# The opening of TensorE in a hybrid mLSTM / attention layer: pinned order, unread products, and the value product between the modulation visits

## The chip, the core and the metric

The kernel runs on one core of a Trainium2 chip. The metric is the device time of one execution in microseconds (us). Of the core's engines, TensorE (PE in the rows; PEld are its weight loads) multiplies, VectorE (DVE), ScalarE (ACT) and GpSimd (POOL) work element by element, and SyncE (SP) issues most of the DMAs. Each engine takes its instructions in the order in which they stand in its queue.

## The reference, cut to what matters

One layer for 512 latent and 128 context tokens, together 640 columns of 1024 features. Only its opening is touched:

```python
mod = (jax.nn.silu(cond) @ w_ada + b_ada)[..., None, :]
sh1, sc1, g1, sh2, sc2, g2 = jnp.split(mod, 6, axis=-1)
h = _rmsnorm(x, norm1_g) * (1 + sc1) + sh1
mq, mk, mv, mo, gates, q_lat, kv_lat, k_rope = _split_cols(h @ w_in, IN_SIZES)
...
```

Behind it come the mLSTM heads, latent attention, the output product and the MLP.

## The kernel before, in words

All matrices are float32. Large products are made of three: a matrix is split into a rounded high part and the low rest, and high x high, low x high and high x low are summed (`mm3`). The splits of weights are `split` (L109 on ScalarE makes the high part `wh`, L110 on VectorE or GpSimd the low part `wl`). Features lie in eight blocks of 128 (k = 0 to 7), tokens in five tiles of 128.

The opening runs so. SyncE fetches x in four pieces, then the first 2048 columns of `w_ada` in eight blocks (`ad`, 1 MB each) with the first weights `st` of the value product between them. ScalarE squares x (L448), VectorE adds the squares in pairs (L449), and TensorE takes their means over features in four groups of five products (`n_pc`, L452; each float32 product of the program shows as two in the trace). GpSimd takes the power -1/2 (`rs`, L361), and TensorE spreads the result over partitions (`n_pb`, L437).

The modulation of the first normalisation comes in four visits, g = 0 to 3. A visit is 16 narrow products (`ada`, L389, "the strips"), a copy of their result by ScalarE (`m`, L394), two products that add the strips up ("the sums", L397), and on VectorE `modT` (L400) and the gain `acol` (L475, L476). Visit g serves blocks k = 2g and 2g+1: VectorE makes `h` (L480), ScalarE its high part `hh` (L481), VectorE its low part `hl` (L482).

Then `group_n` gives the value product `mv`: for each k and each of five tiles the three products L486, L487, L488, 120 in all; after it the product `kv`, 120 again. The program lists the visits first and `mv` after them, and a scheduler, which works with times of its own, sets the order on each engine: what is ready first by its times goes first. Staging tiles `st` come from two buffers, the parts `wh` and `wl` from three each, so the first `kv` weights (`st` of `w_kv`) are fetched into the buffer that the third `mv` pair of blocks leaves once its low part is made.

Of the kernel before, what the change touches and what calls it, by code (L numbers as in the profile page):

```python
# [1 line left out]

# [1 line left out]

# [15 lines left out]
P = 128  # L20
D = 1024
KT = D // P
# [4 lines left out]
NT = T // P  # L27
# [17 lines left out]
ORDER = ("M1", "M6", "M7", "M5", "M2", "M4", "M3")  # L45
ORDER0 = ("M1", "M5", "M2", "M6", "M7", "M4", "M3")
PRE = 4
AHEAD = 2
LAST = 1
OUT_ORDER = (0, 4, 1, 5, 2, 6, 3, 7)  # L50
# [4 lines left out]
def hybrid_layer(ctx: ExitStack, tc: tile.TileContext, d, o):  # L55
    nc = tc.nc
    V, S, G, PE = nc.vector, nc.scalar, nc.gpsimd, nc.tensor
# [41 lines left out]
    def psD(name):  # L99
        return psd.tile([P, 1024], F32, tag="d", name=name)  # L100

    def psS(name):
        return pss.tile([P, 512], F32, tag="s", name=name)
# [226 lines left out]
    ones = const.tile([P, P], F32, name="ones")  # L330
    V.memset(ones, 1.0)
    mean_col = const.tile([P, 2], F32, name="mean_col")
# [4 lines left out]
    small = const.tile([P, 98], F32, name="small")  # L337
# [7 lines left out]
    for what in ORD:  # L345
        if what == "x":
            i = state["x"]
# [34 lines left out]
    V.tensor_scalar(out=sz[:, :, 0:2], in0=sil.rearrange("p (k c) -> p k c", c=2), scalar1=0.5, scalar2=None, op0=ALU.mult)  # L382
    modT = const.tile([P, 48, 2], F32, name="modT")

    def strips(ps, n, q, w):

        for j in range(4):
            k, c = j // 2, slice((j % 2) * n, (j % 2) * n + n)
            PE.matmul(ps[32 * j:32 * j + 32, 0:n], lhsT=sz[:, 2 * q + k, :], rhs=w[:, k, c], start=q == 0, stop=q == 3, tile_position=(0, 32 * j))  # L389

    def mod_cols(n, c0, step, ps):

        rows, pt = Tt(f"m4{c0}", n=n), ps[:, 256:512]
        S.copy(rows, ps[:, 0:n])  # L394
        nb = n // P
        for m in range(nb):
            PE.matmul(pt[:, m * 4:m * 4 + 4], lhsT=rows[:, m * P:(m + 1) * P], rhs=small[:, 94:98], start=True, stop=True)  # L397
        for k in range(2):
            c = slice(c0 + k * step, c0 + k * step + nb)
            V.tensor_tensor(out=modT[:, c, :], in0=pt[:, 0:4 * nb].rearrange("p (m n c) -> p m n c", n=2, c=2)[:, :, k],  # L400
                            in1=bada[:, c].unsqueeze(2).broadcast_to([P, nb, 2]), op=ALU.add)

    fps = {}

    def ada_first(g, q0=0, q1=4):

        if q0 == 0:
            fps[g] = psS(f"ada{g}")
        for q in range(q0, q1):
            strips(fps[g], 256, q, adu[2 * g + q // 2][:, 2 * (q % 2):2 * (q % 2) + 2])  # L410
        if q1 == 4:
            mod_cols(256, 2 * g, 8, fps[g])

    ada_key = iter(ada_order)
    ada_ps = {}
# [13 lines left out]
    def rstd_bc(pc, name):  # L429
        ms = sm("ms", [P, NT], bufs=1)  # L430
        V.tensor_scalar(out=ms, in0=pc, scalar1=EPS, scalar2=None, op0=ALU.add)
        rs = sm("rs", [P, NT], bufs=1)
        rsqrt(rs, ms)
        pbs = [psS(name + "_pb0"), psS(name + "_pb1")]
        dst = [pbs[0][:, i * P:(i + 1) * P] for i in range(4)] + [pbs[1][:, 0:P]]
        for i in range(NT):
            PE.matmul(dst[i], lhsT=rs[:, i:i + 1].broadcast_to([P, P]), rhs=ident, start=True, stop=True)  # L437
        return pbs[0], pbs[1][:, 0:P]
# [1 line left out]
    def xk(k):  # L440
        return x3[k // 4][:, k % 4, :]

    pc = psS("n1_pc")

    for k in range(0, KT, 2):
        sq = [Tt(f"sqx{k + j}") for j in range(2)]
        for j in range(2):
            S.activation(out=sq[j], in_=xk(k + j), func=AF.Square)  # L448
        V.tensor_tensor(out=sq[0], in0=sq[0], in1=sq[1], op=ALU.add)  # L449
        for i in range(NT):  # L450
            c = 5 * k + 2 * i
            PE.matmul(pc[:, c:c + 2], lhsT=sq[0][:, i * P:(i + 1) * P], rhs=mean_col, start=True, stop=True)  # L452
    ms1 = sm("ms1", [P, NT], bufs=1)
    V.tensor_reduce(out=ms1, in_=pc[:, 0:5 * KT].rearrange("p (j i b) -> p i b j", i=NT, b=2)[:, :, 0], axis=AX.X, op=ALU.add)
    ada_first(0, 0, 2)
    ada_first(0, 2, 4)
    rb = rstd_bc(ms1, "n1")
    acol1 = const.tile([P, KT, 2], F32, name="acol1")
    hh = [U("hh0", F32R), U("hh1", F32R)]
    hl = [U("hl0", F32R), U("hl1", F32R)]  # L460
# [1 line left out]
    def kview(us):  # L462
        return [view(us[k // 4], (k % 4) * T, T) for k in range(KT)]

    HH, HL = kview(hh), kview(hl)
    for g in range(4):
        if g:
            ada_first(g)
        if g == 1:
            rbs = Tt("rb1")  # L470
            S.copy(rbs[:, 0:TL], rb[0])
            S.copy(rbs[:, TL:T], rb[1])
            rb = rbs[:, 0:TL], rbs[:, TL:T]
        c2 = slice(2 * g, 2 * g + 2)
        V.tensor_scalar(out=acol1[:, c2], in0=modT[:, 8 + 2 * g:10 + 2 * g, :], scalar1=1.0, scalar2=None, op0=ALU.add)  # L475
        V.tensor_tensor(out=acol1[:, c2], in0=acol1[:, c2], in1=n1g[:, c2].unsqueeze(2).broadcast_to([P, 2, 2]), op=ALU.mult)  # L476
        for k in (2 * g, 2 * g + 1):
            h_ = Pp(f"h_{k}")
            for w, (r_, c) in enumerate(zip(rb, (slice(0, TL), slice(TL, T)))):
                V.scalar_tensor_tensor(out=h_[:, c], in0=xk(k)[:, c], scalar=acol1[:, k, w:w + 1], in1=r_, op0=ALU.mult, op1=ALU.mult)  # L480
                S.activation(out=HH[k][:, c], in_=h_[:, c], func=AF.Identity, bias=modT[:, k, w:w + 1])  # L481
                V.scalar_tensor_tensor(out=HL[k][:, c], in0=h_[:, c], scalar=modT[:, k, w:w + 1], in1=f(HH[k][:, c]), op0=ALU.add, op1=ALU.subtract)  # L482


    def mm3(out, lh, ll, rh, rl, start, stop):
        PE.matmul(out, lhsT=lh, rhs=rh, start=start, stop=False)  # L486
        PE.matmul(out, lhsT=lh, rhs=rl, start=False, stop=False)  # L487
        PE.matmul(out, lhsT=ll, rhs=rh, start=False, stop=stop)  # L488

    def group_n(keys, kts, ncol, name, nada=0):  # L490
        banks = []
        for j in range(2):
            t = psD(f"{name}_{j}")
            banks += [t[:, 0:512], t[:, 512:1024]]
        banks.append(psS(f"{name}_2"))
        k = 0
        for key, nk in zip(keys, kts):
            hi, lo = wget(key)
            for kk in range(nk):
                for i in range(NT):  # L500
                    c = slice(kk * ncol, (kk + 1) * ncol)
                    mm3(banks[i][:, :ncol], HH[k][:, i * P:(i + 1) * P], HL[k][:, i * P:(i + 1) * P], hi[:, c], lo[:, c], k == 0, k == KT - 1)
                k += 1
                if nada and (k - 1) % (2 // nada) == 2 // nada - 1:
                    ada_steps(1)
        return [b[:, :ncol] for b in banks[:NT]]


    ps_mv = group_n([("mv", i) for i in range(4)], (2,) * 4, 512, "mv", 0)
    mv_u = U("mv_u")  # L510
    mv32 = view(mv_u, 0, NT, MH, VC)
    G.memset(mv32[:, :, :, P:VC], 1.0)
# [902 lines left out]
```

## Time and profile before

| | |
|---|---|
| time, median of 3 runs | 885.04 us (884.32 to 886.43) |
| profiled execution, its own time | 885.93 us |
| its span, first to last instruction | 883.8 us |
| TensorE busy | 856.6 us (97% of the span) |
| VectorE / ScalarE / GpSimd busy | 615.9 / 436.6 / 297.2 us |
| chain that ended last, share of TensorE | 84% |

The span is 2.1 us shorter than the execution's time; that rest lies outside the first and last instruction. Busy TensorE in the page counts a product from its start to its modelled end, so cheap and dear products look alike there. All times below are from the start of the span.

### The profile page before, as it was taken

The page shows a single profiled execution, that of the slowest core. Times are in us where ns is not written, and L with a number is a line of the kernel's source. Part 1 is how long each engine was busy: PE and PEld are TensorE (multiplying, and loading weights), DVE is VectorE, ACT ScalarE, POOL GpSimd, SP SyncE. Part 2 cuts the span into 40 slices and gives each one's busy share as a digit, 9 for nine tenths or more (in the row PEclk, how much of TensorE's full clock was granted, in tenths as well). Part 3 has the DMA queues.
Part 4 walks back from the last instruction along what each step waited for, and adds up shares of the span by engine and source line. Part 5 has one row for each costly group of instructions (what it writes and reads, how often), then busy time and mean ns, then how long its engine had stood idle before and what let it go on. Part 6 is the DMA issues. An engine that isn't in the chain of part 4 may idle for free.

```text
span 883.8 us, 15202 instructions
## 1 busy us (share of the span) xinstructions
PE 856.6 (97%) x5805; PEld 801.8 (91%) x5805; DVE 615.9 (70%) x1226; ACT 436.6 (49%) x959; POOL 297.2 (34%) x301
## 2 busy tenths in 40 slices
PE   6999999999889999999989999999999999999998
PEld 5689889999778677889989999999999999999998
DVE  2654733646787889977898587595876949678663
ACT  3424425545864688955557253361544517254540
POOL 3100113322333576743753152241514215152300
PEclk9999999999999999999999999999999999999999
DMA  9742853231316200322141312122122221412132
GB/s 358 307 145 61 281 185 89 63 102 48 99 57 239 96 1 1 120 72 72 49 144 45 99 49 96 49 96 96 49 96 88 80 73 57 134 50 73 48 102 90
DMA packets 22328, 89.63 MB, mean 101 GB/s; under 512 B 3144, under 2 KB 3944, under 8 KB 18928
## 3 DMA queue, kind: packets, MB, share of 16 engines
q1 hardware_dynamic: 19440, 81.95, 26.8%
q0 software_dynamic: 1664, 4.26, 1.7%
q10 hardware_dynamic: 1152, 2.46, 0.7%
q8 instruction: 46, 0.75, 0.4%
q14 instruction: 26, 0.21, 0.1%
HBM read 85.33 MB, written 3.32 MB: 100 GB/s over the span
## 4 chain that ended last, share of the span: by engine, by line
PE 84%; DVE 8%; DMA 3%; ACT 3%; issue 1%; POOL 0%; SPq 0%; DVEq 0%; ACTq 0%; POOLq 0%
PE dn L637 25%; PE qk L637 6%; PE wo L637 5%; PE mo L637 3%; PE ada L389 2%; PE pv L1013 2%; DMA st<-in_w_ada 2%; PE n L702 2%; PE up8M L1235 1%; PE up12M L1235 1%; PE up13M L1235 1%; PE up15M L1235 1%; PE up14M L1235 1%; PE up11M L1235 1%; PE up9M L1235 1%; PE up7M L1235 1%
## 5 line engine op out<-in xcount | busy, mean ns | idle before, releaser
L109 ACT CAST wh<-st 128x1024 fp32r<-128x1024 f32 (+4 forms) x69 | 69.3, 1007 | 101.1 <-PE dn L637 32.9
L1118 DVE SCALAR_TENSOR_TENSOR xr<-dn,modT,xr 128x320 f32<-128x320 f32 x64 | 35.3, 551 | 107.3 <-PE dn L637 107.3
L637 PE MATMUL dn<-fh,wh 128*128 128x320 f32 x448 | 102.7, 310 | 0.2 <-ACT fh L1278 0.2
L110 DVE TENSOR_TENSOR wl<-st,wh 128x1024 fp32r<-128x1024 f32 (+4 forms) x67 | 83.3, 1246 | 27.8 <-ACT wh L109 26.8
L637 PE MATMUL dn<-fh,wl 128*128 128x320 f32 x448 | 102.0, 309 | 0.0
L637 PE MATMUL dn<-fl,wh 128*128 128x320 f32 x448 | 98.7, 309 | 0.0
L109 ACT CAST wu<-S 128x512 fp32r<-128x512 f32 x64 | 38.1, 616 | 98.5 <-issue 92.3
L637 PEld LDWEIGHTS dn<-fh,wh 128*128 128x128 f32 x448 | 74.8, 188 | 2.1 <-PE dn L637 1.6
L637 PEld LDWEIGHTS dn<-fh,wl 128*128 128x128 f32 x448 | 75.0, 188 | 0.0
L637 PEld LDWEIGHTS dn<-fl,wh 128*128 128x128 f32 x448 | 74.1, 188 | 0.0
L1273 POOL TENSOR_TENSOR r<-r,rbs 128x320 f32<-128x320 f32 x32 | 37.4, 1180 | 106.9 <-DVE r L1251 106.9
L110 DVE TENSOR_TENSOR wu<-S,wu 128x512 fp32r<-128x512 f32 x64 | 57.4, 906 | 1.1 <-ACT wu L109 0.9
L1277 ACT ACTIVATE r<-r 128x192 f32<-128x192 f32 (+2 forms) x96 | 40.8, 465 | 26.0 <-DVE r L1251 17.1
L729 POOL TENSOR_TENSOR W<-ngb,mask 128x128 f32<-128x128 f32 x40 | 19.5, 501 | 66.5 <-DVE p L739 33.2
L1280 DVE TENSOR_TENSOR fl<-r,fh 128x320 fp32r<-128x320 f32 x56 | 38.1, 699 | 3.0 <-ACT r L1279 3.0
L1004 POOL TENSOR_TENSOR tot<-tot,p 128x512 f32<-128x512 f32 x24 | 37.2, 1550 | 5.9 <-ACT p L986 3.9
L109 ACT CAST wu<-pair 128x512 fp32r<-128x512 f32 x24 | 14.1, 615 | 43.8 <-PE dn L637 41.6
L110 DVE TENSOR_TENSOR pu<-p,pu 128x512 fp32r<-128x512 f32 x32 | 33.0, 1046 | 2.5 <-ACT pu L109 2.5
L219 POOL TENSOR_TENSOR S<-st,st 128x512 f32<-128x512 f32 x8 | 13.0, 1627 | 60.1 <-DVE wu L110 60.1
L1013 PE MATMUL pv<-pu,v 128*128 128x512 f32 x80 | 29.1, 427 | 2.1 <-DVE pu L110 2.0
L637 PE MATMUL wo<-mh,wh 128*128 128x320 f32 x128 | 29.6, 311 | 0.7 <-DVE xr L1120 0.7
L637 PE MATMUL qk<-hh,wl 128*128 128x320 f32 x128 | 29.9, 312 | 0.0
(487 smaller groups left out, 2437.6 us busy)
## 6 DMA issues: line engine op xcount, KB each, us to landing
st<-in_w_ada SPq DMA_DIRECT2D x16, 1024.0 KB, 5.4
st<-in_w_down SPq DMA_DIRECT2D x32, 512.0 KB, 3.4
ad<-in_w_ada SPq DMA_DIRECT2D x8, 1024.0 KB, 17.2
st<-in_w_up SPq DMA_DIRECT2D x16, 512.0 KB, 3.7
pair<-in_w_up SPq DMA_DIRECT2D x16, 512.0 KB, 4.9
st<-in_w_qko SPq DMA_DIRECT2D x12, 512.0 KB, 3.6
st<-in_w_out SPq DMA_DIRECT2D x8, 512.0 KB, 3.5
x<-in_x SPq DMA_DIRECT2D x4, 640.0 KB, 6.8
```

The lines of the kernel that those rows point to most:

```text
L109: S.copy(hi, src)
L110: return eng.tensor_tensor(out=lo, in0=src, in1=f(hi), op=ALU.subtract)
L389: PE.matmul(ps[32 * j:32 * j + 32, 0:n], lhsT=sz[:, 2 * q + k, :], rhs=w[:, k, c], start=q == 0, stop=q == 3, tile_position=(0, 32 * j))
L637: PE.matmul(out[:, hf * 512:hf * 512 + HT], lhsT=wt[:, c], rhs=xt[k][:, hf * HT:(hf + 1) * HT], start=k0 == 0 and n == 0, stop=k1 == nk an ...
L729: G.tensor_tensor(out=W[:, dg:dg + P], in0=nb_[dr][:, j * P:(j + 1) * P], in1=mask[:, dr, :], op=ALU.add)
L1004: G.tensor_tensor(out=tot[h], in0=first, in1=pj, op=ALU.add)
L1013: PE.matmul(pacc[h], lhsT=v_u[hf][:, j, hh_, :], rhs=w, start=j == 0 and k == 0, stop=j == 4 and k == 1)
L1118: V.scalar_tensor_tensor(out=xr[m][:, 0:HT], in0=ps[:, 0:HT], scalar=modT[:, gi_ + m, 0:1], in1=xr[m][:, 0:HT], op0=ALU.mult, op1=ALU.add)
L1235: PE.matmul(ps, lhsT=w[:, c], rhs=b[k], start=k == 0 and w is hi and b is bh, stop=k == 3 and w is lo)
L1273: E.tensor_tensor(out=t, in0=t, in1=rbs[:, c], op=ALU.mult)
L1277: S.activation(out=t[:, c0:c1], in_=t[:, c0:c1], func=AF.Relu, bias=r[n][:, w:w + 1])
L1280: V.tensor_tensor(out=FL[n][:, c], in0=t, in1=f(FH[n][:, c]), op=ALU.subtract)
```

## The change

Three things, all in the opening. First, `spin(n)` issues n products of a block of ones with itself into a PSUM tile `idle` that nothing reads: 18 before the first mean group, 5, 4 and 2 between the groups, 3 between the halves of the first visit's strips, 1 before its sums and 6 after them. Second, a chain (`queued`, `line["pe"]`) makes the scheduler issue TensorE's instructions of the opening in the order of the program. Third, `mv` is written between the visits: ahead of a visit's strips go four tiles of the block before, behind them the fifth tile, then the visit's sums, then the next block.

```diff
+SPIN = (18, 5, 4, 2, 3, 6)
...
+    def queued():
+        return tc.issue_after(line["pe"].ins) if "pe" in line else nullcontext()
+
+    def spin(n):
+
+        with queued():
+            for _ in range(n):
+                line["pe"] = PE.matmul(idle[:, 0:P], lhsT=ones, rhs=ones, start=True, stop=True)
...
-        if q1 == 4:
+    def ada_sums(g):
+        with queued():
             mod_cols(256, 2 * g, 8, fps[g])
+        line["pe"] = line["sums"]
...
-    pc = psS("n1_pc")
+    pc, idle = psS("n1_pc"), psS("idle")
+    spin(SPIN[0])
...
+        if k < KT - 2:
+            spin(SPIN[1 + k // 2])
...
     ada_first(0, 0, 2)
+    spin(SPIN[4])
     ada_first(0, 2, 4)
-    rb = rstd_bc(ms1, "n1")
+    with queued():
+        rb = rstd_bc(ms1, "n1")
+    spin(1)
+    ada_sums(0)
+    spin(SPIN[5])
...
+    mvt = [psD("mv_0"), psD("mv_1")]
+    ps_mv = [t[:, c:c + 512] for t in mvt for c in (0, 512)] + [psS("mv_2")]
...
+    def mv_tiles(k, tiles):
+        if k % 2 == 0 and k not in mv_w:
+            mv_w[k] = wget(("mv", k // 2))
+        hi, lo = mv_w[k - k % 2]
+        c = slice(k % 2 * 512, k % 2 * 512 + 512)
+        with queued():
+            for i in tiles:
+                line["pe"] = mm3(ps_mv[i], HH[k][:, i * P:(i + 1) * P], HL[k][:, i * P:(i + 1) * P], hi[:, c], lo[:, c], k == 0, k == KT - 1)
+
     for g in range(4):
         if g:
+            mv_tiles(2 * g - 2, range(4))
             ada_first(g)
+            mv_tiles(2 * g - 2, range(4, NT))
+            ada_sums(g)
+            mv_tiles(2 * g - 1, range(NT))
...
-    ps_mv = group_n([("mv", i) for i in range(4)], (2,) * 4, 512, "mv", 0)
+    for k in (KT - 2, KT - 1):
+        mv_tiles(k, range(NT))
+    line.pop("pe")
```

The order on TensorE from its first product to the first value product, before (names as above; the number behind a name is the buffer's):

```order
L452 MATMUL n_pc<-mean_col,sqx_178 128x2 x5
L389 MATMUL ada_190<-ad_113,sz 32x256 x8
L389 MATMUL ada_190<-ad_115,sz 32x256 x8
L437 MATMUL n_pb_217<-ident,rs 128x128 x4
L437 MATMUL n_pb_218<-ident,rs 128x128
L397 MATMUL ada_190<-small,m_207 128x4 x2
L389 MATMUL ada_245<-ad_119,sz 32x256 x8
L389 MATMUL ada_245<-ad_121,sz 32x256 x8
L486 MATMUL mv_365<-wh_368,hh_225 128x512
```

The same stretch of the changed kernel, from the last mean group on:

```order
L472 MATMUL n_pc<-mean_col,sqx_208 128x2 x5
L402 MATMUL ada_220<-ad_113,sz 32x256 x8
L396 MATMUL idle<-ones 128x128 x3
L402 MATMUL ada_220<-ad_115,sz 32x256 x8
L455 MATMUL n_pb_244<-ident,rs 128x128 x4
L455 MATMUL n_pb_245<-ident,rs 128x128
L396 MATMUL idle<-ones 128x128
L410 MATMUL ada_220<-small,m_252 128x4 x2
L396 MATMUL idle<-ones 128x128 x6
L495 MATMUL mv_269<-wh_288,hh_265 128x512
```

The strips of the visit g = 1 (`ada_245` before) have left the place ahead of the first value product; in the changed kernel they stand behind twelve value products, the four tiles of k = 0.

TensorE in the changed kernel around the sums of the visit g = 3 (`ada_465`). Ahead of these rows stand its strips, the fifth tile of k = 4 and six more products of `kv` like the first three here:

```order
L495 MATMUL kv_567<-wh_449,hh_265 128x304
L496 MATMUL kv_567<-wl_450,hh_265 128x304
L497 MATMUL kv_567<-wh_449,hl_267 128x304
L410 MATMUL ada_465<-small,m_485 128x4 x2
L495 MATMUL mv_269<-wh_296,hh_266 128x512
L496 MATMUL mv_269<-wl_297,hh_266 128x512
L497 MATMUL mv_269<-wh_296,hl_268 128x512
```

Nine products of `kv`, which need the first `kv` weights, now stand ahead of this visit's sums; before, the sums stood among products of `mv`, and the nine came 19 products later.

ScalarE in the changed kernel from the third visit's copy to the fourth's:

```order
L407 COPY m_410<-ada_390 128x256 [waits PE_49,Activation_49]
L110 CAST wh_296<-st_129 128x1024 [waits DMAHW7_49]
L532 ACTIVATE hh_266<-h_433,modT 128x512 [waits DMAHW0_49,DVE_49]
L532 ACTIVATE hh_266<-h_433,modT 128x128 [waits DVE_49]
L110 CAST wh_374<-st_135 128x1024 [waits DMAHW0_49,Pool_49]
L532 ACTIVATE hh_266<-h_440,modT 128x512 [waits DVE_49]
L532 ACTIVATE hh_266<-h_440,modT 128x128 [waits DVE_49]
L110 CAST wh_449<-st_372 128x912 [waits DMAHW2_49,PE_49,Pool_49]
L407 COPY m_485<-ada_465 128x256 [waits PE_49]
```

The high part of the first `kv` weights (`wh_449`) now stands ahead of the fourth visit's copy; before it stood behind it. On VectorE the low part of the third `mv` weights (`wl_297`) now comes ahead of the first `hl` of k = 4, where it came behind it. GpSimd and SyncE keep their order, and so does every engine behind the end of `kv`.

## Rows read from the trace of the kernel before

**Rows 1.** The page: TensorE's busy tenths and clock by slices, the last chain by engine.

```profile
PE   6999999999889999999989999999999999999998
...
PEclk9999999999999999999999999999999999999999
...
PE 84%; DVE 8%; DMA 3%; ACT 3%; issue 1%; POOL 0%; SPq 0%; DVEq 0%; ACTq 0%; POOLq 0%
```

**Rows 2.** Timeline of TensorE, 0 to 25 us: start, duration, what, count, idle before.

```profile
7.76 8.75 PE L452 MATMUL n_pc<-mean_col,sqx 128*128 128x2 f32 x40 [7.76 <-DVE sqx L449]
16.44 3.64 PE L389 MATMUL ada<-ad,sz 128*32 128x256 f32 x32
20.01 2.50 PE L437 MATMUL n_pb<-ident,rs 128*128 128x128 f32 x10
22.30 0.56 PE L397 MATMUL ada<-small,m 128*128 128x4 f32 x4
22.79 1.93 PE L389 MATMUL ada<-ad,sz 128*32 128x256 f32 x32
```

**Rows 3.** Timeline of TensorE, 459 to 467 us: the same shapes in the second normalisation.

```profile
459.33 1.17 PE L1211 MATMUL n_pc<-mean_col,accx 128*128 128x2 f32 x10
...
465.78 1.27 PE L437 MATMUL n_pb<-ident,rs 128*128 128x128 f32 x10
```

**Rows 4.** Timeline of VectorE, 12 to 25 us.

```profile
12.68 0.83 DVE L449 TENSOR_TENSOR sqx<-sqx,sqx 128x640 f32<-128x640 f32 x1 [0.73 <-ACT sqx L448]
16.55 0.18 DVE L454 TENSOR_REDUCE ms<-n_pc 128x5 f32<-128x20 f32 x1 [3.04 <-PE n_pc L452]
...
22.97 0.23 DVE L400 TENSOR_TENSOR modT<-ada,small 128x4 f32<-128x4 f32 x2 [6.04 <-PE ada L397]
...
23.64 1.92 DVE L480 SCALAR_TENSOR_TENSOR h<-x,acol,n_pb 128x512 f32<-128x512 f32 x4
```

**Rows 5.** Timeline of ScalarE, 17 to 21 us.

```profile
17.47 1.04 ACT L109 CAST wh<-st 128x1024 fp32r<-128x1024 f32 x1 [4.83 <-DMA st<-in_w_mv]
20.14 0.37 ACT L394 COPY m<-ada 128x256 f32<-128x256 f32 x1 [1.63 <-PE ada L389]
```

**Rows 6.** DMA issues, 4.1 to 4.4 us (second `ad` block): size, time to landing.

```profile
ad<-in_w_ada SPq DMA_DIRECT2D x1, 1024.0 KB, 12.2
```

**Rows 7.** Timeline of GpSimd, 12 to 31 us.

```profile
17.02 1.20 POOL L361 TENSOR_TENSOR rs<-ms,mhalf 128x5 f32<-128x5 f32 x1 [12.28 <-DVE ms L431]
18.59 2.35 POOL L110 TENSOR_TENSOR wl<-st,wh 128x1024 fp32r<-128x1024 f32 x1 [0.36 <-ACT wh L109]
28.29 2.38 POOL L110 TENSOR_TENSOR wl<-st,wh 128x1024 fp32r<-128x1024 f32 x1 [7.34 <-ACT wh L109]
```

**Rows 8.** Timeline of VectorE in the visit g = 1.

```profile
30.05 0.64 DVE L475 TENSOR_SCALAR acol<-modT 128x4 f32<-128x4 f32 x1
...
30.97 1.94 DVE L480 SCALAR_TENSOR_TENSOR h<-x,acol,rb 128x512 f32<-128x512 f32 x4
```

**Rows 9.** Timeline of TensorE: first value product, and the last two.

```profile
25.20 0.50 PE L486 MATMUL mv<-wh,hh 128*128 128x512 f32 x1 [0.47 <-ACT hh L481]
...
59.95 0.39 PE L487 MATMUL mv<-wl,hh 128*128 128x512 f32 x1
60.18 0.39 PE L488 MATMUL mv<-wh,hl 128*128 128x512 f32 x1
```

**Rows 10.** Timeline of VectorE, 38 to 49 us.

```profile
38.54 1.94 DVE L480 SCALAR_TENSOR_TENSOR h<-x,acol,rb 128x512 f32<-128x512 f32 x4
...
41.06 1.22 DVE L110 TENSOR_TENSOR wl<-st,wh 128x1024 fp32r<-128x1024 f32 x1
...
47.43 1.11 DVE L110 TENSOR_TENSOR wl<-st,wh 128x912 fp32r<-128x912 f32 x1 [2.21 <-ACT wh L109]
```

**Rows 11.** Timeline of ScalarE: the first `kv` weights.

```profile
46.44 0.95 ACT L109 CAST wh<-st 128x912 fp32r<-128x912 f32 x1 [2.48 <-DMA st<-in_w_kv]
```

**Rows 12.** DMA issues, 40 to 46 us: median time to landing.

```profile
st<-in_w_kv SPq DMA_DIRECT2D x2, 456.0 KB, 3.7
```

More of the change, by code (lines that the diff above doesn't have):

```diff
@@ L1 @@
-from contextlib import ExitStack
+from contextlib import ExitStack, nullcontext
 import numpy as np
@@ L383, in hybrid_layer @@
     modT = const.tile([P, 48, 2], F32, name="modT")
+    line = {}
+    def queued():
[4 more added lines that the diff above has]
+                line["pe"] = PE.matmul(idle[:, 0:P], lhsT=ones, rhs=ones, start=True, stop=True)
     def strips(ps, n, q, w):
@@ L388, in strips @@
             k, c = j // 2, slice((j % 2) * n, (j % 2) * n + n)
-            PE.matmul(ps[32 * j:32 * j + 32, 0:n], lhsT=sz[:, 2 * q + k, :], rhs=w[:, k, c], start=q == 0, stop=q == 3, tile_position=(0, 32 * j))
+            line["strip"] = PE.matmul(ps[32 * j:32 * j + 32, 0:n], lhsT=sz[:, 2 * q + k, :], rhs=w[:, k, c], start=q == 0, stop=q == 3, tile_position=(0, 32 * j))
     def mod_cols(n, c0, step, ps):
@@ L396, in mod_cols @@
         for m in range(nb):
-            PE.matmul(pt[:, m * 4:m * 4 + 4], lhsT=rows[:, m * P:(m + 1) * P], rhs=small[:, 94:98], start=True, stop=True)
+            line["sums"] = PE.matmul(pt[:, m * 4:m * 4 + 4], lhsT=rows[:, m * P:(m + 1) * P], rhs=small[:, 94:98], start=True, stop=True)
         for k in range(2):
@@ L408, in ada_first @@
             fps[g] = psS(f"ada{g}")
-        for q in range(q0, q1):
-            strips(fps[g], 256, q, adu[2 * g + q // 2][:, 2 * (q % 2):2 * (q % 2) + 2])
-        if q1 == 4:
+        with queued():
+            for q in range(q0, q1):
+                strips(fps[g], 256, q, adu[2 * g + q // 2][:, 2 * (q % 2):2 * (q % 2) + 2])
+                line["pe"] = line["strip"]
+    def ada_sums(g):
+        with queued():
             mod_cols(256, 2 * g, 8, fps[g])
+        line["pe"] = line["sums"]
     ada_key = iter(ada_order)
@@ L449, in hybrid_layer @@
         V.tensor_tensor(out=sq[0], in0=sq[0], in1=sq[1], op=ALU.add)
-        for i in range(NT):
-            c = 5 * k + 2 * i
-            PE.matmul(pc[:, c:c + 2], lhsT=sq[0][:, i * P:(i + 1) * P], rhs=mean_col, start=True, stop=True)
+        with queued():
+            for i in range(NT):
+                c = 5 * k + 2 * i
+                last = PE.matmul(pc[:, c:c + 2], lhsT=sq[0][:, i * P:(i + 1) * P], rhs=mean_col, start=True, stop=True)
+        line["pe"] = last
+        if k < KT - 2:
+            spin(SPIN[1 + k // 2])
     ms1 = sm("ms1", [P, NT], bufs=1)
@@ L455, in hybrid_layer @@
     ada_first(0, 0, 2)
+    spin(SPIN[4])
     ada_first(0, 2, 4)
-    rb = rstd_bc(ms1, "n1")
+    with queued():
+        rb = rstd_bc(ms1, "n1")
+    spin(1)
+    ada_sums(0)
+    spin(SPIN[5])
     acol1 = const.tile([P, KT, 2], F32, name="acol1")
@@ L465, in hybrid_layer, with mm3 @@
     HH, HL = kview(hh), kview(hl)
+    def mm3(out, lh, ll, rh, rl, start, stop):
+        PE.matmul(out, lhsT=lh, rhs=rh, start=start, stop=False)
+        PE.matmul(out, lhsT=lh, rhs=rl, start=False, stop=False)
+        return PE.matmul(out, lhsT=ll, rhs=rh, start=False, stop=stop)
+    mvt = [psD("mv_0"), psD("mv_1")]
+    ps_mv = [t[:, c:c + 512] for t in mvt for c in (0, 512)] + [psS("mv_2")]
+    mv_w = {}
+    def mv_tiles(k, tiles):
[3 more added lines that the diff above has]
+        c = slice(k % 2 * 512, k % 2 * 512 + 512)
+        with queued():
+            for i in tiles:
+                line["pe"] = mm3(ps_mv[i], HH[k][:, i * P:(i + 1) * P], HL[k][:, i * P:(i + 1) * P], hi[:, c], lo[:, c], k == 0, k == KT - 1)
     for g in range(4):
         if g:
+            mv_tiles(2 * g - 2, range(4))
             ada_first(g)
+            mv_tiles(2 * g - 2, range(4, NT))
+            ada_sums(g)
+            mv_tiles(2 * g - 1, range(NT))
         if g == 1:
@@ L482, in hybrid_layer @@
                 V.scalar_tensor_tensor(out=HL[k][:, c], in0=h_[:, c], scalar=modT[:, k, w:w + 1], in1=f(HH[k][:, c]), op0=ALU.add, op1=ALU.subtract)
[L485 to L488, printed above, removed]
     def group_n(keys, kts, ncol, name, nada=0):
```

## The prediction, on record before the changed kernel ran

> **What bounds the kernel now.** I read the page first. TensorE's busy tenths are 9 in nearly every slice behind the opening, and the last chain lies on TensorE for 84% [rows 1]. A microsecond that TensorE gains or loses in the opening therefore mostly stays to the end, and the question is when its last value product ends: at 60.2 + 0.23 = 60.4 us, one product after the start of the last row, since products of this shape follow each other by 60.18 - 59.95 = 0.23 us [rows 9].
>
> The timeline of the opening comes second [rows 2]. From 7.76 to about 22.7 us TensorE is busy without a gap, but slowly. The 32 strip products of the first visit take 3.64 us, the 32 of the second 1.93; the ten `n_pb` products take 2.50 us, and the same ten 1.27 at 466 us; forty mean products take 8.75 us, while ten take 1.17 later [rows 2, 3]. [...]
>
> Third, the wait ahead of `mv`: VectorE gets the first visit's sums for `modT` at 22.97, makes `h` from 23.64, and TensorE's first value product starts at 25.20 [rows 4, 9]. The second visit's strips (22.79, 1.93 us) fill that wait [rows 2]; before's idle stretch ahead of 25.20 is 0.47 us [rows 9].
>
> **The start of `mv`, term A.** The unread products begin as soon as the block of ones is set, in the second microsecond. Eighteen of them are 36 in the trace; at the slow spacing of 8.75/40 = 0.22 us that is 7.9 us, at the fast one of 1.17/10 = 0.12 about 4.2, so they end between about 5.3 and 9 us, around the 7.76 at which the first mean group could start. I take the clock as risen by then, since 6 us of wide products raised it before. The last square sum is ready at 12.68 + 0.83 = 13.5 [rows 4]; its mean group ends at 14.7 instead of 16.5. The reduction, the power on GpSimd (1.20 us, ready 1.7 us after the means, as 18.2 after 16.55) are done by 16.4 [rows 4, 7]. The second `ad` block lands at about 16.2, 12.2 us after an issue just ahead of 4.1 [rows 6]; even if both halves of the strips waited for it, they would end at 16.2 + 1.9 = 18.1. So no unread product stands in anybody's way: strips and the ten `n_pb` products are done between 18.4 and 19.4.
>
> Now the next wait. The copy of the strips stands behind the first weight cast on ScalarE, which waits for its DMA until 17.47 and takes 1.04 [rows 5]. The copy (0.37) ends at 18.9, and `modT` follows about 0.9 later (0.67 from the start of the sums, and their weight load), at 19.8 [rows 2, 4, 5]. Behind it `acol` wants to run while GpSimd makes the low part of that same weight block, 18.59 to 20.94 [rows 7]. In the second visit of before just this happened: `acol` took 0.64 us and ended at 30.69, GpSimd's 28.29 + 2.38 = 30.67 [rows 7, 8]. I read that as VectorE held until GpSimd was through. The gain is then ready at 20.95; `h` starts 0.28 later (30.97 after 30.69) [rows 8], and the first value product 1.56 after that (25.20 after 23.64) [rows 4, 9]: at 22.8. **A is 2.4 us gained.** Without the hold it would be 21.95, that is 3.2; that is the upper bound. The lower one is 1.3, should the ten `n_pb` products still run slowly: 18.1 + 2.5, 0.9 to `modT` at 21.5, its 2.2 us to the first value product as before (25.20 after 22.97), so 23.7 to 23.9.
>
> **What follows the start.** The work from there to the last `mv` product is the same, plus what left the idle time ahead of it. *B*: the second visit's strips now stand behind twelve value products: 1.93 us lost [rows 2]. They cost nothing before because the wait for `h` covered them; that cover is gone. *C*: on VectorE the low part of the third weight pair now comes ahead of the first `hl` of k = 4. Counted from the start of the third visit's sums: `modT` 0.9, first `h` 0.67 later, four `h` 1.94, so the low part runs from 3.5 to 4.7 (1.22) [rows 4, 10]. TensorE needs 0.5 for the sums and 15 x 0.23 = 3.5 for k = 3, does two products with the high part, and wants the low part at 4.5; then `hl`, some 0.7 us of VectorE after 4.7. **C is 0.4 lost**, 0 to 0.7.
>
> *D*: the fourth visit's sums stand behind nine `kv` products, whose weights are fetched into the buffer that the low part of C releases at 4.7. They land 3.7 us later (median of two) [rows 12], are cast in 0.95 [rows 11] and lowered in 1.11 [rows 10]: 10.5. TensorE, behind 15 products of k = 4 (3.5) and the strips (1.93) and C, is there at 9.9. **D is 0.5 lost**; 0 at the fast end, 1.0 if the transfer is like the first one, whose cast began 4.16 us after the low part's end at 42.28 [rows 10, 11]. The nine products themselves are only moved.
>
> Later visits stand later than before, so their `ad` blocks have landed; the other queues keep their order, and the rest shifts as a whole. The last value product would end at 60.4 - 2.4 + 1.9 + 0.4 + 0.5 = 60.8: **0.4 us later**, and the profiled execution's 885.93 would become 886.3.
>
> That execution is 0.89 us above the median of its runs, 885.04. Its ten `n_pb` products at the low level cost it 2.50 - 1.27 = 1.2 us [rows 2, 3]; an execution whose clock rises sooner has not that loss, and the changed kernel's opening has it in neither case. What the 0.89 is the trace does not tell. I take half of it as common to both kernels and half as this loss, and forecast 886.3 - 0.4 = 885.9 us. That is 0.1% above the median, while a measurement of this kernel tells some 0.2% (1.8 us) from no change.
>
> [...]
>
> **Rivals.** *The early start is kept* (faster). If neither C nor D waits and VectorE is not held, the last product ends 3.2 - 1.9 = 1.3 us earlier, 884.6, still inside 0.2%. To pass it B must hide too, which needs TensorE idle again behind 22.8: then the profiled 885.93 loses up to 3.2 and the time is about 882.8. For it speaks that the scheduler of before may have left waits that I count as busy; against it, no idle time stands at the value products' rows beyond 0.47 us [rows 9].
>
> *The fourth visit waits for `kv`* (slower). Sums, `modT`, `h` and the blocks k = 6 and 7 all stand behind those weights, and TensorE has nothing else queued. Each microsecond by which they land later than 3.7 us after the release is a microsecond lost. From 4.6 on the time passes 886.8; at 5.7 it is 887.9. For it: 4.16 has been seen with an idle queue [rows 10, 11]. Against: the other one was faster, the median being 3.7.
>
> *The unread products do not lift the clock*, or do not keep it up between the mean groups. Then they only stand in the way: 36 + 62 products at 0.22 us end the means at 22.7 instead of 16.5, strips and unread ones take 5 us, `n_pb` 2.5, and `mv` starts near 33.5; with B that is 10 us more, 896. Against it: before's `n_pb`, the same width, ran ahead of the rise.
>
> **Chances.** My sum with its bounds 0.62; start kept 0.14; `kv` wait 0.20; clock 0.04. My sum's own range, from A 3.2 and no waits (1.7 us below the forecast) to A 1.3 with C 0.7 and D 1.0 (1.9 above), is 884.2 to 887.8. For 8 in 10 I give 883.6 to 887.8; beyond it lie most of the start-kept case, part of the `kv` wait and the clock. Nearly all of my sum lies within 0.2% (883.3 to 886.8): 0.62. Faster 0.14, slower 0.24.
>
> **What would show it.** Right: wide unread products from the second microsecond with the spacing halving before 9 us; the last mean group ending near 14.7; `acol` of the first visit ending with GpSimd's low part near 20.9; first value product near 22.8; two TensorE waits, 0.4 us at the first products of k = 4 and 0.5 at the second `kv` product; last value product near 60.8. Wrong: `acol` in 0.17 us beside a busy GpSimd (A too small), strips 1 starting after a wait, `kv` weights landing over 4.6 us after their release, mean groups that still take 2 us, or a change behind 76 us, where no order moved.

## The result, and the profile of the changed kernel

| | before | changed |
|---|---|---|
| time, median | 885.73 us (883.84 to 890.36, 8 runs) | 893.31 us (889.56 to 895.70, 8 runs) |
| profiled execution: its time, its span | 885.93, 883.8 us | 891.57, 889.8 us |

The changed kernel is slower: ratio 1.0071, 95% interval 1.0053 to 1.0090. The forecast was 885.9 us with a range up to 887.8, so the prediction was wrong. Its direction, a little slower, came true; the loss is 7.6 us where it had less than 1.

The page of the changed kernel, to be read beside [rows 1] (first TensorE's line of busy time and instructions, which stood in the table before only as its time, then the slices and a DMA queue):

```profile
PE 865.7 (97%) x5883; PEld 810.4 (91%) x5883; DVE 616.2 (69%) x1226; ACT 436.8 (49%) x959; POOL 297.1 (33%) x301
...
PE   9999999999989899999989999999999999999998
...
PEclk7999999999999999999999999999999999999999
...
q8 instruction: 46, 0.75, 0.4%
```

TensorE is fuller than before in the first slice (9 tenths against 6), and its granted clock there reads lower (7 against 9). Before, TensorE showed 5805 products and as many weight loads; 5883 of each are 156 instructions more, the 39 unread products. The line q8 (a DMA queue: packets, MB, share) will matter: the instructions themselves come by DMA, 0.75 MB in 46 packets, which is 16 KB each.

The timeline of TensorE in the changed kernel, which answers to [rows 2, 9]:

```profile
1.06 5.93 PE L396 MATMUL idle<-ones 128*128 128x128 f32 x36 [1.06 <-DVE ones L332]
7.76 1.28 PE L472 MATMUL n_pc<-mean_col,sqx 128*128 128x2 f32 x10 [0.78 <-DVE sqx L468]
8.90 1.36 PE L396 MATMUL idle<-ones 128*128 128x128 f32 x10
10.10 1.18 PE L472 MATMUL n_pc<-mean_col,sqx 128*128 128x2 f32 x10
11.13 1.85 PE L396 MATMUL idle<-ones 128*128 128x128 f32 x8
12.78 2.13 PE L472 MATMUL n_pc<-mean_col,sqx 128*128 128x2 f32 x10
...
15.76 2.13 PE L472 MATMUL n_pc<-mean_col,sqx 128*128 128x2 f32 x10
17.82 1.93 PE L402 MATMUL ada<-ad,sz 128*32 128x256 f32 x16
...
26.68 0.50 PE L495 MATMUL mv<-wh,hh 128*128 128x512 f32 x1 [0.89 <-ACT hh L532]
29.82 1.93 PE L402 MATMUL ada<-ad,sz 128*32 128x256 f32 x32
```

The first two mean groups take 1.28 and 1.18 us, the fast duration of [rows 3]; the third and fourth take 2.13. The granted clock by stretches says the same (columns: stretch, its length, busy time of the five engines, clock, DMA share, GB/s):

```profile
8.00:12.00 4.00, 4.00 (x35) 4.00 (x35) 1.58 (x2) 3.13 (x6) 0.00 (x0) 0.92 1.03 398
12.00:16.00 4.00, 4.00 (x21) 4.00 (x21) 0.90 (x2) 0.67 (x2) 0.00 (x0) 0.50 1.01 418
16.00:20.00 4.00, 4.00 (x26) 2.71 (x27) 0.35 (x2) 0.96 (x1) 1.20 (x1) 0.50 1.03 426
20.00:25.00 5.00, 5.00 (x45) 4.08 (x45) 0.47 (x4) 0.45 (x2) 2.35 (x1) 0.84 1.01 418
25.00:30.00 5.00, 4.11 (x24) 2.85 (x26) 3.87 (x9) 2.88 (x5) 1.14 (x1) 1.00 1.01 421
```

So the unread products did lift the clock before 8 us (granted 1.00 from 4.5 us on), but it fell to 0.50 at 11.4 us (0.92 in the stretch from 8 to 12), among the two-column mean products and the unread ones between them, while TensorE had no idle time, and stayed low until 21.6 (0.84 from 20 to 25). In that time unread products run at the slow spacing too (six in the trace take 1.65 us from 19.68 on, where ten took 1.36 from 8.90 on), and stand in the way. `mv` starts at 26.68 instead of 25.20. (Stretches ahead of the first change of the clock read 1.00, those from 8 to 16 us in before too, where that change is at 22.4 and the mean products stand 0.22 us apart [rows 2]; there the spacing of products is the better witness.)

The second thing that this opening shows is on the queues. DMA queues of the changed kernel from 14 to 18 us:

```profile
q8 instruction: 1, 0.02, 1.7%
```

One instruction packet travels here among the weight transfers; the same stretch of before has none. Of the 16 engines' time the weights' queue q1 has 99.1% here, where it has 100.9% in before. The second `ad` block landed some 1.7 us later than before (17.9 instead of 16.2), and the cast of the first weights on ScalarE, 17.47 before [rows 5], starts at 19.04:

```profile
19.04 1.04 ACT L110 CAST wh<-st 128x1024 fp32r<-128x1024 f32 x1 [6.37 <-DMA st<-in_w_mv]
```

The trace keeps sixteen landing signals for each such transfer, as many as the core has DMA engines. Fifteen of this block's came by 16.16 us, no later than in before (16.18), and the last alone at 17.91. The blocks queued behind it lag in the same way; the first weights have fifteen signals by 17.40 and the last at 19.01.

Because everything came late, VectorE was not held: `acol` took 0.17 us, where [rows 8] show 0.64, since GpSimd's low part had ended at 22.5. VectorE in the changed kernel:

```profile
24.72 0.17 DVE L526 TENSOR_SCALAR acol<-modT 128x4 f32<-128x4 f32 x1
...
25.13 1.92 DVE L531 SCALAR_TENSOR_TENSOR h<-x,acol,n_pb 128x512 f32<-128x512 f32 x4
```

Third, behind the opening. The last `kv` product, in before and then in the changed kernel:

```profile
75.71 0.30 PE L488 MATMUL kv<-wh,hl 128*128 128x304 f32 x1
```

```profile
79.26 0.30 PE L497 MATMUL kv<-wh,hl 128*128 128x304 f32 x1
```

By here 3.55 us are lost. But the span is 6.0 longer, so another 2.45 are lost behind this row, where no order was moved. TensorE's waits from 76 to 320 us (total, times, longest) show where part of the rest goes, before and then changed:

```profile
PE ada L389 <- DMA st<-in_w_ada: 1.4, 3, 0.7
```

```profile
PE ada L402 <- DMA st<-in_w_ada: 3.0, 3, 1.2
```

Two of these waits, near 280 and 300 us, before and then changed:

```profile
275.63 1.07 PE L389 MATMUL ada<-st,sz 128*32 128x256 f32 x16 [0.47 <-DMA st<-in_w_ada]
294.64 1.07 PE L389 MATMUL ada<-st,sz 128*32 128x256 f32 x16 [0.16 <-DMA st<-in_w_ada]
```

```profile
280.16 1.07 PE L402 MATMUL ada<-st,sz 128*32 128x256 f32 x16 [1.19 <-DMA st<-in_w_ada]
299.99 1.07 PE L402 MATMUL ada<-st,sz 128*32 128x256 f32 x16 [1.01 <-DMA st<-in_w_ada]
```

The later visits' weights arrive late, though nothing in their program changed. The waits for them grew by 3.0 - 1.4 = 1.6 of the 2.45 us.

### The profile page after: what moved, and what is told of

Its sections match the earlier page's. It is cut to its first block, busy times and chain, and to the rows that moved or that the text cites. A ratio compares the mean times of both kernels' runs of the same rounds, so it can differ in the third digit from the quotient of the medians.

```text
span 889.8 us, 15359 instructions
## 1 busy us (share of the span) xinstructions
PE 865.7 (97%) x5883; PEld 810.4 (91%) x5883; DVE 616.2 (69%) x1226; ACT 436.8 (49%) x959; POOL 297.1 (33%) x301
## 4 chain that ended last, share of the span: by engine, by line
PE 85%; DVE 7%; DMA 3%; ACT 3%; issue 2%; SPq 0%; DVEq 0%; ACTq 0%
PE dn L685 25%; PE qk L685 6%; PE wo L685 5%; PE mo L685 3%; PE ada L402 2%; DMA st<-in_w_ada 2%; PE n L750 2%; PE pv L1061 2%; PE up12M L1283 1%; PE up8M L1283 1%; PE up4M L1283 1%; PE up14M L1283 1%; PE up15M L1283 1%; PE up7M L1283 1%; PE up3M L1283 1%
## 5 line engine op out<-in xcount | busy, mean ns | idle before, releaser
L220 POOL TENSOR_TENSOR S<-st,st 128x512 f32<-128x512 f32 x8 | 13.5, 1682 | 59.2 <-DVE wu L111 59.2
```

## The experiments

All kernels compute the whole reference. Ratios are to the kernel before, run on the same chip.

**First: the unread products, or the order?** Theory 1: the clock falls among the narrow mean products, and the unread ones get in the way. Theory 2: the order alone (strips behind twelve value products, sums behind `kv`) costs all.

*No unread products, the rest of the change kept:*

```diff
-SPIN = (18, 5, 4, 2, 3, 6)
+SPIN = (0, 0, 0, 0, 0, 0)
...
-    spin(1)
     ada_sums(0)
```

> The changed kernel without any unread product; the pinned order and the value product between the visits stay. Theory 1 (the clock: the unread products lift it near 4.5 us, it falls again at 11.4 while narrow mean products run, and from there the unread products only stand in the way, at the low level): the opening goes as before the change, first value product at 25 to 25.5 us; the strips behind it (1.9) and the waits at k = 4 and at the kv products (0.3 and 1.2) stay, last value product near 63.9, time about 889, 0.4% over before and 4 us under the changed kernel. Theory 2 (the order alone: the strips and the sums behind the kv products cost all of it, the clock nothing): the time of the changed kernel, 893.

Measured 888.55 us, before 887.21; ratio 1.0025 (1.0010 to 1.0041). Its `mv` starts at 24.61, earlier than in before, but with a wait that the strips no longer fill:

```profile
24.61 0.79 PE L494 MATMUL mv<-wh,hh 128*128 128x512 f32 x1 [2.33 <-ACT hh L531]
```

In its profile the clock fell there, from 24.5 to 27.9 us, and the first value products came some 0.43 us apart instead of 0.23.

*The opening only: unread products and pinned order up to the first value product, `mv` as before:*

```diff
     spin(SPIN[5])
+    line.pop("pe")
...
-    for k in (KT - 2, KT - 1):
-        mv_tiles(k, range(NT))
+    ps_mv = group_n([("mv", i) for i in range(4)], (2,) * 4, 512, "mv", 0)
```

> The unread products and the pinned order as far as the first value product; behind it the visits and the value product are scheduled as before the change. Theory 1: the clock falls near 11 us as in the changed kernel, first value product near 26.7 (1.5 late), nothing lost behind it: 887 to 888. Theory 2: no loss, 885.7.

Measured 891.94, ratio 1.0066 (1.0042 to 1.0090): almost the whole loss, well above what theory 1 gave it. In its profile the first value product is at 25.10, where before has 25.20, and the last `kv` product at 77.41, 1.7 us late; the scheduler left half of the second visit's strips behind value products here. By the two runs theory 2 falls as the whole cause; the unread products are most of it, but by more than the opening explains.

*Mean products of 128 columns instead of 2, in the changed kernel and in the one before* (same instructions, overlapping columns, the same ones read):

```diff
-    PE.matmul(pc[:, c:c + 2], lhsT=sq[0][:, i * P:(i + 1) * P], rhs=mean_col, start=True, stop=True)
+    PE.matmul(pc[:, c:c + P], lhsT=sq[0][:, i * P:(i + 1) * P], rhs=mean_w, start=True, stop=True)
```

> The changed kernel with mean products of 128 columns instead of 2 (the same values, in 128 columns of which one is read; a product costs its weight load either way). Theory 1: the wide columns keep the clock up behind 11 us, a mean group takes 1.1 to 1.2 us throughout, the means end near 14.8 instead of 17.9, first value product near 22.8 instead of 26.7; about 889.5, some 3.5 under the changed kernel. Theory 2: 893, as the changed kernel.

> The kernel before with mean products of 128 columns and nothing else. Theory 1: wide products from 7.8 us on lift the clock by about 15 us instead of 22.4; strips and n_pb run fast, first value product 23 to 24 instead of 25.2, and the second visit's strips stay in idle time: 883.5 to 885, that is 0.1 to 0.2% faster. Theory 2: 885.7, no change, since the clock of the opening does not matter.

Measured 894.32, ratio 1.0070 (1.0043 to 1.0097), and 887.07, ratio 1.0006 (0.9990 to 1.0022). The clock did what theory 1 says. The changed kernel with wide mean products, by stretches:

```profile
12.00:16.00 4.00, 4.00 (x44) 3.29 (x43) 1.18 (x3) 0.57 (x1) 0.48 (x1) 1.00 1.01 418
16.00:20.00 4.00, 4.00 (x42) 3.30 (x42) 0.15 (x2) 1.42 (x2) 1.07 (x2) 1.00 1.02 424
20.00:25.00 5.00, 2.38 (x14) 2.00 (x13) 4.89 (x10) 1.96 (x5) 2.00 (x1) 0.89 1.01 416
25.00:30.00 5.00, 5.00 (x42) 3.27 (x41) 1.03 (x3) 0.91 (x1) 2.37 (x1) 0.77 1.02 424
```

It is full from 8 to 20 us, through all mean groups (1.28 us each, where one of two columns takes 1.18 at the full clock), and the first value product starts at 23.81:

```profile
23.81 0.75 PE L497 MATMUL mv<-wh,hh 128*128 128x512 f32 x1 [2.62 <-ACT hh L534]
24.36 0.63 PE L498 MATMUL mv<-wl,hh 128*128 128x512 f32 x1
24.78 0.63 PE L497 MATMUL mv<-wh,hh 128*128 128x512 f32 x1
```

But TensorE had then idled 2.62 us, the clock fell once more (0.89 from 20 to 25, 0.77 from 25 to 30), and value products came 0.42 us apart instead of 0.23. And the time did not change. So theory 1 has the clock right and the loss wrong. (In the kernel before, the edit does not single out the clock: the scheduler's order changed with it, and half of the second visit's strips went behind 15 value products. Its `mv` starts at 23.11, as theory 1 had it, but the clock was low again from 34.4 to 37.8, and the last `kv` product is at 77.63, 1.9 us late.)

**Second: the instruction packets.** The traces of these kernels show the packets on q8 each time TensorE has taken some 256 instructions (before: 2 x 5805 in 46 packets, 252 each), in all of them at about the same places of its queue; 156 more at the front move every later one to an earlier place of the program. In the changed kernel and in the two others with all 39 unread products one fell on the transfer for the first `ada` visit behind the opening, issued near 88 to 92 us, which took 6.4 to 6.5 us; without them it took 4.7 to 4.9. It marks the packets well, but costs nothing itself: no wait of TensorE for `ada` weights stands between 76 and 104 us in any of these traces. The waits near 280 and 300 us above do cost, and in the changed kernel a packet falls into each of the two transfers, at 277.3 and 295.6 us. That is theory 3. Four kernels test it, and one tests term B.

*Before, with as many instructions, but tiny, in TensorE's idle front; then with a whole packet of them:*

```diff
+    for _ in range(39):        # 64 in the second kernel
+        PE.matmul(idle[0:2, 0:2], lhsT=ones[:, 0:2], rhs=ones[:, 0:2], start=True, stop=True)
```

> The kernel before, with one addition: 39 unread products of 2 weight columns and 2 moving columns at TensorE's front, where it idles until 7.7 us. They are as many TensorE instructions (156) as the 39 unread products of the change, but the order behind them and the value product are those of before. Theory 3 (code fetches): the traces show TensorE's code arriving in 16 KB packets on the engines that carry the weight transfers, one each 256 instructions; 156 more of them at the front move every later packet earlier, as in the changed kernel one fell at 15.8 us beside the second ada block, at 91.7 beside an ada transfer that then took 6.5 us instead of 4.9, and at 295.6 beside another (5.5 instead of 4.7). It expects this kernel 2 to 4 us slower than before, 888 to 890, with the transfer issued near 89 us taking over 6 us. Theory 1 (the unread products are in the way between the mean groups and the clock falls among them): nothing stands between the mean groups here, so as before, 885 to 886. Theory 2 (the order of strips and value products): as before too.

> As the kernel before this one, but with 64 such small unread products, 256 TensorE instructions, which is one whole code packet: every packet behind the opening should fall where it falls in the kernel before, and one more falls in the opening. Theory 3: the transfers near 89 and near 290 us take as long as before (4.9 and 4.7), and only the opening can lose, by one packet of some 1 us: 885.5 to 887.5, faster than the 39 small products although there are more of them. A rival to it, that unread products cost by their number: slower than the 39. Theories 1 and 2: as before, 885 to 886, if the 64 end by 7.7 us.

Measured on one chip, before 886.25: with 156 instructions 890.19, ratio 1.0042 (1.0024 to 1.0060); with 256 only 887.49, ratio 1.0012 (0.9989 to 1.0036). More products cost less in the median, by 2.7 us: it is not their number, though the two intervals overlap. TensorE takes the rest of its products in the order of before in both. With 156 the opening is as before, by the value products (durations, then first and last start):

```profile
L490 PE MATMUL mv<-wh,hl x40: 388/396/504, 26.1 to 60.0; 128*128 128x512 f32 x40
```

They start from 26.3 to 60.2 in before. What changes lies behind it: TensorE's waits from 76 to 320 us (1.4 in before), the two that cost most of it, the DMA queues from 87 to 95 us, and the issue at 87.8 (median us to landing last):

```profile
PE ada L389 <- DMA st<-in_w_ada: 3.7, 4, 1.0
```

```profile
277.04 1.07 PE L389 MATMUL ada<-st,sz 128*32 128x256 f32 x16 [1.04 <-DMA st<-in_w_ada]
296.77 1.07 PE L389 MATMUL ada<-st,sz 128*32 128x256 f32 x16 [0.92 <-DMA st<-in_w_ada]
```

```profile
q8 instruction: 1, 0.02, 0.7%
```

```profile
st<-in_w_ada SPq DMA_DIRECT2D x1, 1024.0 KB, 6.8
```

In before that transfer took 4.9. With 256 instructions it takes 4.8 again, at 88.2, and of the two waits the second alone is left:

```profile
st<-in_w_ada SPq DMA_DIRECT2D x1, 1024.0 KB, 4.8
```

```profile
295.03 1.07 PE L389 MATMUL ada<-st,sz 128*32 128x256 f32 x16 [0.41 <-DMA st<-in_w_ada]
```

In all four kernels with 156 more instructions a packet falls into the transfer for which TensorE waits near 300 us, and the wait is 0.84 to 1.02 us; in the ten others it is 0.53 or less. In two of the four (the opening only, and the wide mean products) the clock fell there as well, for 6.8 us from 300 on.

*The changed kernel with its unread products filled up to one packet:*

```diff
-    spin(SPIN[5])
+    with queued():
+        for _ in range(31):
+            line["pe"] = PE.matmul(idle[0:2, 0:2], lhsT=ones[:, 0:2], rhs=ones[:, 0:2], start=True, stop=True)
```

> The changed kernel with its last six unread products (ahead of the first value product) replaced by 31 of 2 weight columns and 2 moving columns, so that the unread products are 256 TensorE instructions instead of 156. The opening up to there is unchanged, its code packet at 15.8 us too. Theory 3: the packets behind the opening fall as in the kernel before, the transfers near 91 and 294 us take 4.9 and 4.7 us again, and 2 to 3 us of the changed kernel's loss go: 890 to 891.5. Theories 1 and 2: as the changed kernel, 893 to 894, or up to 1 us more if the 31 small ones take longer than the idle time.

Measured 889.75, ratio 1.0035 (1.0013 to 1.0057), where the changed kernel has 1.0071: half of the loss goes by adding instructions. Not all of that need be the packets: in its profile the clock rose later than in the changed kernel's (6.9 us instead of 4.5), was low from 13.7 to 20.6, and `mv` started at 25.17 instead of 26.68. The wait and the transfer at 90.1 us are back to the kernel before:

```profile
PE ada L402 <- DMA st<-in_w_ada: 1.4, 3, 0.9
```

```profile
st<-in_w_ada SPq DMA_DIRECT2D x1, 1024.0 KB, 4.7
```

*No unread products, and the second visit's strips ahead of `mv`:*

```diff
         if g:
+            if g == 1:
+                ada_first(g)
             mv_tiles(2 * g - 2, range(4))
-            ada_first(g)
+            if g > 1:
+                ada_first(g)
```

> The pinned order without any unread product, as in the first experiment of this study, but the second visit's strips ahead of the first value products instead of behind twelve of them. The prediction's term B says that this gives 1.93 us back, since TensorE waits there for the modulated columns anyway: 886 to 887 where the same without this edit took 888.55 (before: 887.2 on that chip). The rival, that the value product pinned tile by tile costs elsewhere (weights that land late, visits behind kv products): no change, 888 to 889.

Measured 885.37, ratio 0.9994 (0.9973 to 1.0015), against 1.0025 for the same without this edit. That is 0.3% or 2.7 us for one place in the queue, and term B's 1.93 lies inside what the intervals leave. The rest may be the low clock behind the unfilled wait of 2.33 us, which is gone too: no product of this `mv` lasts over 0.50 us, where the slow ones without this edit last 0.63. TensorE there:

```profile
22.01 1.93 PE L402 MATMUL ada<-ad,sz 128*32 128x256 f32 x32
24.41 0.50 PE L494 MATMUL mv<-wh,hh 128*128 128x512 f32 x1 [0.47 <-ACT hh L534]
```

The strips fill the wait again that they filled before [rows 2, 9].

**Third: does it add up, and is the clock worth anything?** Before is 886.11 us on this chip.

*The changed kernel with both repairs (the two diffs above), and the same with wide mean products:*

> The changed kernel with two repairs: the unread products made 256 TensorE instructions instead of 156, as in the run before, and the second visit's strips ahead of the first value products. If the losses add up (term B 1.9 us, the code packets 3.1 us), what is left is that the unread products and the low clock among the mean groups hold up the opening: 887 to 888.5, a ratio of 1.001 to 1.003. If the strips' place gave nothing in this opening, because TensorE comes late anyway: 889.5.

> As the one before, with 128 columns in the mean products. In the changed kernel these kept the clock up through all mean groups (6.8 to 23.9 us). If the low clock is what is left of the loss: the first value product near 24, and 885.5 to 887, a ratio of 0.999 to 1.001. If the clock of the opening is worth nothing here: as the one before, 887 to 888.5.

Measured 887.07, ratio 1.0007 (0.9987 to 1.0027), and 886.93, ratio 1.0011 (0.9994 to 1.0028). The two repairs take nearly all of the 0.71%. With wide mean products the granted clock reads 1.00 in every stretch up to 30 us; these are a stretch, the wait ahead of the value product on TensorE, and the gain on VectorE:

```profile
16.00:20.00 4.00, 4.00 (x50) 3.22 (x47) 0.02 (x1) 1.42 (x2) 0.84 (x1) 1.00 1.01 420
```

```profile
23.95 1.07 PE L404 MATMUL ada<-ad,sz 128*32 128x256 f32 x16 [1.35 <-DMA ad<-in_w_ada]
24.95 0.50 PE L499 MATMUL mv<-wh,hh 128*128 128x512 f32 x1
```

```profile
20.24 2.19 DVE L533 TENSOR_SCALAR acol<-modT 128x4 f32<-128x4 f32 x1
```

```profile
20.05 2.35 POOL L111 TENSOR_TENSOR wl<-st,wh 128x1024 fp32r<-128x1024 f32 x1 [3.21 <-ACT wh L110]
```

This is the opening that the prediction drew, without a slow product in it, but for the strips' place: `modT` is there at 20.2, and `acol` is held until GpSimd's low part ends at 22.4. The strips wait for their second block until 23.95, and `mv` starts at 24.95, 0.25 us before the kernel before. Both delays hang on the packet at 15.8 us, which this opening shares with the changed kernel: fifteen of the block's landing signals came by 22.43 and the last at 23.91, and the first weights landed at 18.91 instead of 17.45. Transfers and the hold set the start, and the clock gives nothing back.

*No unread products, strips first, wide mean products:*

> The pinned order without unread products and with the second visit's strips first, and the mean products with 128 columns instead of 2 (they write overlapping columns, of which the same two are read). With the wide ones the clock rose at 13.9 us instead of 22.4 in the kernel before, and no TensorE instruction is added, so no code packet moves. If TensorE's clock in the opening is worth time: the first value product at about 23.6 instead of 24.4, the kv products' end near 74.5 instead of 75.3, and 0.5 to 1 us faster than the same with narrow ones, a ratio to before of 0.998 to 0.999. The rival (the strips wait for their second block, which lands at 22.4 in any case, and GpSimd's copy holds VectorE): no difference, 0.999 to 1.000.

Measured 886.08, ratio 0.9995 (0.9979 to 1.0011): no difference to narrow ones, the rival's case. The run does not say what a clock that stays up would give: in its profile the clock rose at 11.7 us but was low again from 21.9 to 28.7, behind two waits of the strips for their blocks (1.13 and 1.34 us). `mv` started at 24.33, with its first products 0.43 us apart, and the last `kv` product is at 76.58, where the kernel with narrow ones has 75.00.

*No unread products of full size, strips first, and 26 tiny ones (104 instructions) at the front* (the diff of the tiny ones above):

> The pinned order without the unread products and with the strips first, with 26 small unread products (104 TensorE instructions) at the idle front. Theory 3: nothing in the opening's order changes, but every code packet comes 104 instructions earlier, so that one falls near 91 us beside an ada transfer and one near 294 beside another, about as with 156: 1.5 to 3 us slower than without them, 887 to 888.5, a ratio of 1.001 to 1.003 instead of 0.9994. The rival (only the 39 products' number, or one place that 104 does not hit): 885 to 886.

Measured 886.49, ratio 1.0005 (0.9991 to 1.0020): a miss for my placing of the packets. The profile says why: the packet came at 92.0 us, just when the transfer issued at 87.3 had landed (4.7 us), and fell on the next one, issued at 88.2 (8.6 us instead of 7.7 in the kernel without the 104); TensorE waits for neither. Two other packets do fall into transfers for which it waits, at 111.4 and 293.8 us, but these waits are 0.36 and 0.49 us, where the kernel without the 104 has none and 0.53.

So theory 3 holds in its mechanism: what a packet costs hangs on the transfer on which it falls, and when. I could not place it by counting instructions. Over all kernels: with 156 more instructions the four ratios are 1.0042 to 1.0071, with 256 more 1.0007 to 1.0035, with none 0.9994 to 1.0025.

## Why the prediction was wrong, point by point

- **Term A is the step that failed**, at "I take the clock as risen by then" and "no unread product stands in anybody's way". The first was right for 8 us and not for 12: the clock went down among the narrow mean groups. The two speeds that the forecast reckoned with stand in the traces as granted clocks: in before 1.00 from 22.4 us on, in the changed kernel 1.00 from 4.5, 0.50 from 11.4 and 1.00 again from 21.6. `mv` started at 26.68 where the forecast had 22.8 and its worst bound 23.9: 1.5 us lost instead of 2.4 gained. The 1.5 is one execution's size. In the two other profiles with this opening (the opening only, and the one filled up to 256) the clock rose at 6.7 and 6.9 us instead of 4.5, was low for 6.8 us instead of 10.2, and `mv` started at 25.10 and 25.17: nothing gained and nothing lost. The third rival had named it ("do not keep it up between the mean groups"), at 4% and with too high a price of 10 us. The second block's late landing, at 17.91, has no share in the 1.5: TensorE was busy with slow products until it came to that half of the strips at 21.26. It is the clock that lost here, but a clock that stays up gives only 1.4 of the 2.4 us, by the changed kernel with wide mean products, where it was up until `mv` started, at 23.81. The hold of `acol` was there as drawn, but ended 1.07 us later than the forecast 20.95, since the first weights, behind the code packet, reached ScalarE's cast at 18.53 instead of 17.47:

```profile
18.53 1.04 ACT L110 CAST wh<-st 128x1024 fp32r<-128x1024 f32 x1 [0.22 <-DMA st<-in_w_mv]
20.12 1.90 DVE L528 TENSOR_SCALAR acol<-modT 128x4 f32<-128x4 f32 x1
```

- **Term B** was right: 1.93 us in the changed kernel's row, and 0.3% by undoing it, with and without unread products (1.0025 to 0.9994, and 1.0035 to 1.0007), within wide intervals.
- **C and D** were about 0.2 us and nearly 0 in place of 0.4 and 0.5. For C, the two products with the low part start from 46.39 on and the next one at 47.05, which is 0.66 us for two where 0.46 is the spacing. For D, the sums start at 53.04, 0.14 behind the ninth `kv` product, which is the spacing of these. The `kv` weights landed 3.2 us after their issue, so the second rival's case did not come.
- **A term was missing**, and it is the largest, at "the other queues keep their order, and the rest shifts as a whole". No queue's order changed, yet TensorE's instructions are themselves a transfer on the same DMA engines (46 packets of 16 KB; one of them took 1.7% of the 16 engines' time from 14 to 18 us), and 156 more at the front moved every later packet of it against the weights. By the kernel with the 156 tiny ones this costs 0.42%, 3.7 us, with the opening untouched. In its profile, whose span is 3.3 us longer, 2.3 are waits for `ada` weights; where the rest arises was not traced. Filling the changed kernel's up to 256 gives 0.36% back, part of which may be its opening's.
- **The sum, as measured**: in the profiled execution 1.5 (A) + 1.9 (B) + 0.2 (C) = 3.6 us up to the end of `kv`, as the rows at 75.71 and 79.26 have it, and 2.45 behind it. Of the 7.6 us between the medians, B, C and 3.7 for the packets make 5.8, and A adds between nothing and 1.5: 5.8 to 7.3. That this comes so near is in part luck, since A, B and C are read from single executions. What the prediction called a sign of error ("mean groups that still take 2 us", "a change behind 76 us") are the two that appeared.
- Settled in part: how a packet of 16 KB delays a transfer of 1 MB. With the 156 tiny ones, fifteen of the sixteen landing signals of the transfer issued at 87.8 came within 4.72 us, as in before (4.73), and the last alone at 6.80 instead of 4.88. One part in sixteen is late, and the transfer with it. Not settled: why it is late by 1.5 to 2.1 us in the four kernels when the packet took 0.9 to 1.1, and why some packets cost nothing: in before one started at 267.9, behind an issue at 267.6, and that transfer took 4.8 us.

## What to carry to other kernels

Count an added instruction twice: in its engine's time, and in the stream of code, which shared the DMA engines with the weights here; when a small edit moves the time far away from where it was made, compare the places of the instruction packets and the times to landing before looking for a cause in the order. To test for it, pad the edit up to a whole packet of instructions and see whether the loss goes. And work that is put "between" is free only where something else is waited for at that moment: the strips' place cost nothing in front of the value product and nearly 2 us behind it.

## What the hardware showed that I had not expected

- **Code packets.** Code came in packets of 16 KB (0.75 MB in 46 packets), one for some 252 TensorE instructions in before and 256 in the changed kernel. No row above shows TensorE waiting for its code, but a transfer with a packet inside it landed later: the one issued near 88 to 92 us took 6.4 to 6.8 us instead of 4.7 to 5.0, in the four kernels with a packet inside that transfer and in none of the others.
- **The clock falls without idle time.** In the changed kernel the granted clock was 0.50 from 12 to 16 us, with TensorE busy throughout 8 to 16 us. The fall behind the 2.62 us wait above had idle time ahead of it, in which TensorE waited for ScalarE. In the three other kernels with these narrow products behind unread ones it fell too, at 13.5, 13.7 and 15.6 us; in the two with 128 columns in place of 2 in the same instructions it did not fall there.
- **The clock falls far from the opening too, in some executions.** Near 454 us, where TensorE waits shortly between the first `up` products of the MLP, the kernel with the strips first had half the clock, and lost some 2 us there (40.4 us from its first `up` product to its first `dn` product, 38.3 in before):

```profile
454.00:461.00 7.00, 6.24 (x24) 5.43 (x22) 4.97 (x10) 2.06 (x4) 1.38 (x1) 0.52 0.00 1
```

  The kernel before has full clock in that slice [rows 1]. A single profile can differ from the next by 2 us for that reason alone, which is why every comparison above is of medians.
